# An encoder layer's bias-mask fill in four parts, and its output projection with operands two entries ahead, squares on ScalarE, sums by matmuls and other PSUM banks

## The chip, the cores and the metric

The kernel runs on one core of a Trainium2 chip. The metric is the device time of one execution in microseconds (us), as a median over several runs.

Engines are named as the profile names them: PE is TensorE (PEld its weight loads), DVE is VectorE, ACT is ScalarE, POOL is GpSimd, SP is SyncE, which issues the DMAs. PSUM, into which PE writes, has eight banks, numbered 0 to 7 here.

## The reference

One layer is computed for two batches that share the weights: 1024 tokens (`x_sample`) and 256 tokens (`x_prompt`), 1024 features, in float32.

```python
x = x + 0.5 * rmsnorm(swiglu(rmsnorm(x, ffn1_pre), ffn1_w_gu, ffn1_w_down), ffn1_post)
h = rmsnorm(x, mix_pre)
qa, ka, va, qb, kb, vb = jnp.split(h @ w_in, ...)
oa = window_gqa(rope(qa), rope(ka), va, sink_a)          # A: +-128 tokens, 8 heads on 2 kv heads
ob = neighbourhood_attn(qb, kb, vb, rpb_b)               # B: 8 x 16 window of a 64-wide grid, relative bias
mix = jnp.concatenate([rmsnorm(oa, out_norm_a), rmsnorm(ob, out_norm_b)], axis=-1) @ w_out
x = x + rmsnorm(mix, mix_post)
x = x + 0.5 * rmsnorm(swiglu(rmsnorm(x, ffn2_pre), ffn2_w_gu, ffn2_w_down), ffn2_post)
x = rmsnorm(x, final_norm)
```

`rmsnorm(x, g)` is `x * rsqrt(mean(x*x) + 1e-6) * g`. `swiglu(x)` is `(silu(x @ w_gate) * (x @ w_up)) @ w_down` with 2816 hidden features. Attention B adds a bias table where a key lies in the query's window and −1e30 elsewhere.

## The kernel before

**The numbers' form.** Each float32 operand of a product is split in two (`split`): a rounded part `h` and the rest `l`. A product is three matmuls, `h·h`, `h·l` and `l·h`, summed in PSUM. So each operand costs a copy on ACT and a subtraction on DVE ahead of PE.

**The order.** The program runs in stages: FFN1 (gate and up, then down), the mixer's projections and attentions A and B, the mixer output, FFN2 (gate and up, then down). Each engine has a queue of its own and works it off in order. The order on the queues is written by the code, by small planners (`pipe.start` gives a step's parts due times, `pipe.run` calls them between products) and by a tile scheduler that may move instructions within what the data allow. A tile's buffer is taken again only when its last reader is done, and a PSUM bank likewise.

**FFN gate and up** (`GateUp`). For each of 22 column blocks `f` and both row chunks, seven products (L324) go to four accumulators per chunk, with the tags `A0` to `A3` and `B0` to `B3` on banks 0 to 7. ACT and DVE turn them into hidden tiles `w` and `v` (two buffers each; L333 is the addition that starts `v`, L336 the copy that starts `u`). `store` writes them to DRAM as `hd` over SP (L357). While step `f` runs, `load` fetches the weights of a later one (L273), and `prep` splits them.

**The bias tables** (`bias_tables`). While FFN1 runs, each step `f` from 2 on calls one entry of a list, placed behind the last weight load of that step. Six `skew` steps write the tables `zd` and `zp` to DRAM. Then `fill_neg` writes the mask value −1e30 over all of `ttp` (2048 rows of 256 values, L500), and the steps after it copy table rows into `tt` (L488) and `ttp`.

**The down weights** (`wd_first`). Ahead of step 21 of either FFN the first weights of the down product are loaded (`rawd`) and split. The scheduler places these loads much earlier: beside step 8 in FFN1 and at the start of FFN2.

**Row factors.** `square` sums a row's squares on ACT (L194), `row_factor` makes `rsqrt(sum / 1024 + 1e-6)` of one or two such sums with small POOL instructions (L204 adds two sums, L206, L207). At the end of either FFN, two sums come together.

**The mixer output** (`MixOut`). Its work is ten entries, each two tiles of 128 rows for one attention: `(8,A), (0,A), (8,B), (2,A), (0,B), (4,A), (2,B), (6,A), (4,B), (6,B)`. `operands` loads the attention's output (tile `ml`, L984), makes `mh` by four ACT copies (L989), the squares by one DVE multiplication (L990) and two additions (L994, L995), and `ml` by four DVE instructions (L992). Two matmuls against a column of ones (L1000) give the rows' sums, and L1002 and L1003 make the row factor `ro` of them. `product` (L1015) makes a tile's half of 512 columns with twelve matmuls. `done` takes it from PSUM: for A an ACT copy into `y` (L1027), for B a DVE instruction that adds it to `y` (L1036). After B come the norms, the residual on POOL (L1042), the stores of `x2d` (L1044) and of the normalised tile `xnd` (L1048).

Entries 0 and 1 run inside the last attention head. `run` does entries 2 to 9, and starts the operands of entry n+1 with entry n. Beside entries 8 and 9 it calls steps of FFN2's preparation: `fetch2` loads tiles of `xnd` (L1316), `blocks` (L241 to L260) transposes and combines them, `gu.prep(0)` splits the first weights. The accumulators `y` have banks 0 to 4, the transposes and sums (tag `tr`) 6, 7 and 5.

Of the kernel before, what the change touches and what calls it, by code (L numbers as in the profile page):

```python
# [34 lines left out]
def third(t):  # L35
    return (t // 4, (t % 4) * 128) if t < 8 else (2, (t - 8) * 128)
# [31 lines left out]

def rstd(c, src_list, n):

    nc = c.nc
    ss = c.small.tile([128, 2], F32, name="ss")
    for i, s in enumerate(src_list):
        junk = c.junk.tile([128, s.shape[1]], BF16, name="junk", bufs=1)
        nc.scalar.activation(junk, s, AF.Square, accum_out=ss[:, i:i + 1])
    r = c.small.tile([128, 1], F32, name="rs")
    if len(src_list) == 2:
        s2 = c.small.tile([128, 1], F32, name="ss2")
        nc.gpsimd.tensor_tensor(s2, ss[:, 0:1], ss[:, 1:2], op=ALU.add)
    else:  # L80
        s2 = ss[:, 0:1]
    nc.gpsimd.tensor_scalar(r, s2, 1.0 / n, EPS, op0=ALU.mult, op1=ALU.add)
    nc.gpsimd.tensor_tensor(r, r, c.mhalf, op=ALU.pow)
    return r
# [17 lines left out]
def new_xt(c):  # L102
# [7 lines left out]
def norm_to_xt(c, x, gain, xt, t, xn=None):  # L110

    nc = c.nc
    r = rstd(c, [x], D)
    yield
    if xn is None:
        xn = c.work.tile([128, D], F32, name="xn")
    nc.vector.scalar_tensor_tensor(xn, x, r, gain, op0=ALU.mult, op1=ALU.mult)
    yield
    th, off = third(t)
    yield from transpose_split(c, xn, xt[0][th][:, :, off:off + 128], xt[1][th][:, :, off:off + 128])  # L120

# [69 lines left out]
def square(c, x, junk):  # L191

    ss = c.small.tile([128, 1], F32, name="ss")
    c.nc.scalar.activation(junk[:, :x.shape[1]], x, AF.Square, accum_out=ss)  # L194
    return ss


def row_factor(c, sums):

    nc = c.nc  # L200
    r = c.small.tile([128, 1], F32, name="rs")
    s = sums[0]
    if len(sums) == 2:
        nc.gpsimd.tensor_tensor(r, sums[0], sums[1], op=ALU.add)  # L204
        s = r
    nc.gpsimd.tensor_scalar(r, s, 1.0 / D, EPS, op0=ALU.mult, op1=ALU.add)  # L206
    nc.gpsimd.tensor_tensor(r, r, c.mhalf, op=ALU.pow)  # L207
    return r
# [168 lines left out]
class Down:  # L377
# [49 lines left out]
    def first_done(self, t, pool, junk):  # L427
        c, nc = self.c, self.c.nc
        ps = self.ps.pop(t)
        ss = self.ssq[:, t:t + 1]  # L430
        nc.scalar.activation(junk[:, :512], ps, AF.Square, accum_out=ss)
        y = pool.tile([128, 512], F32, name="y0")
        nc.vector.tensor_copy(y, ps)
        nc.sync.dma_start(self.y0d[t], y)
        self.ss[t] = ss
# [18 lines left out]
def bias_tables(c, G, rpb, cmask, neg, tt, ttp, zd, zp):  # L454
# [43 lines left out]

    def fill_neg():
        nc.sync.dma_start(ttp.rearrange("a n q h e k -> (a n q h) (e k)"), neg.to_broadcast([2048, 256]))  # L500

    steps = [lambda tau=tau, g=g: skew(g, tau) for g in range(2) for tau in range(3)]
    steps.append(lambda: (fill_neg(), fill(0, 0)))
    fills = [lambda a=a, rh=rh: fill(a, rh) for a in range(8) for rh in range(2)][1:]
# [411 lines left out]
class MixOut:  # L916
# [13 lines left out]
    def open(self):  # L930
# [7 lines left out]
        self.ones = wp.tile([128, 1], F32, name="ones")  # L938
        nc.gpsimd.memset(self.ones, 1.0)
        self.a = self.L.open("woa", 1)  # L940
# [32 lines left out]
    def prep(self, n):  # L973
        if n < len(self.seq):
            self.c.pipe.start(self.operands(*self.seq[n]), self.PREP)

    def operands(self, t, half):

        c, nc, a = self.c, self.c.nc, self.a
        lo = a.tile([128, 4, 256], F32R, name="ml", bufs=2)  # L980
        o = lo.bitcast(F32)
        src = self.oAd[:, :, t * 128:t * 128 + 256] if half == 0 else \
            (self.oBd[0][:, :, t * 128:t * 128 + 256] if t < 8 else self.oBd[1])
        nc.sync.dma_start(o, src.rearrange("j p t -> p j t"))  # L984
        yield
        hi = a.tile([128, 4, 256], F32R, name="mh", bufs=2)
        sq = a.tile([128, 4, 256], F32, name="sq")
        for j in range(4):
            nc.scalar.activation(hi[:, j], o[:, j], AF.Copy, scale=self.gon[:, 4 * half + j:4 * half + j + 1])  # L989
        nc.vector.tensor_tensor(sq, o, o, op=ALU.mult)  # L990
        for j in range(4):
            nc.vector.scalar_tensor_tensor(lo[:, j], o[:, j], self.gon[:, 4 * half + j:4 * half + j + 1], hi[:, j].bitcast(F32),  # L992
                                           op0=ALU.mult, op1=ALU.subtract)
        nc.vector.tensor_tensor(sq[:, 0:2], sq[:, 0:2], sq[:, 2:4], op=ALU.add)  # L994
        nc.vector.tensor_tensor(sq[:, 0], sq[:, 0], sq[:, 1], op=ALU.add)  # L995
        self.ops[t, half] = (hi, lo)
        yield
        ps = c.ps.tile([128, 2], F32, name="ssq", tag="tr")
        for i in range(2):
            nc.tensor.matmul(ps[:, i:i + 1], sq[:, 0, i * 128:i * 128 + 128], self.ones, start=True, stop=True)  # L1000
        r = c.small.tile([128, 2], F32, name="ro")
        nc.vector.tensor_scalar(r, ps, 1.0 / 512, EPS, op0=ALU.mult, op1=ALU.add)  # L1002
        nc.gpsimd.tensor_tensor(r, r, c.mhalf.to_broadcast([128, 2]), op=ALU.pow)  # L1003
        self.r[t, half] = r
# [45 lines left out]
    def run(self, G, beside):  # L1050

        c = self.c
        self.gmp = load_gain(c, G, self.g_mp, "ga")
        self.gf2 = load_gain(c, G, self.g_f2, "gb")
        for n in range(2, len(self.seq)):
            self.prep(n + 1)
            side = beside(n)
            for i in range(2):
                fill = []
                for s in range(2):  # L1060
                    fill.append((2.6, lambda s=s: self.product(n, i, s)))
                    fill += [(0.0, st) for st in side[2 * i + s::4]]
                c.pipe.run([[]], fill)
# [9 lines left out]
def encoder(tc, i, out_p, out_s):  # L1073
# [208 lines left out]
    def finish1(t, x, gain):  # L1282
# [7 lines left out]
        for _ in transpose_split(c, xn, state["xt"][0][th][:, :, off:off + 128], state["xt"][1][th][:, :, off:off + 128]):  # L1290
# [142 lines left out]
```

## Time and profile before

| | us |
|---|---|
| median of 3 runs | 2430.55 (2429.84 to 2431.99) |
| the profiled execution | 2433.46 |
| its span, from first to last instruction | 2431.4 |
| FFN1 gate and up, one step undisturbed | 24.63 |
| FFN1 gate and up, longest step | 42.66 |
| entries 2 to 9 of the mixer output (1419.0 to 1534.6 in the span) | 115.6 |
| from there to FFN2's second step (1534.6 to 1619.6) | 85.0 |

The profile's mean granted clock of PE was 0.983 of full speed. A line of the profile names engine, program line and operation with `output<-inputs`, counts (`x`), and times; in a timeline the first two numbers are the start in us from the span's start and the duration in us, and square brackets hold the idle time before the instruction and what ended it. In a row of windows each engine has its busy time and, in brackets, its instructions; the last three numbers are the granted clock, the DMA engines' busy share and GB/s.

### The profile page before, as it was taken

What the parts mean: (1) busy time and instruction counts of PE and PEld (TensorE: products, weight loads), DVE (VectorE), ACT (ScalarE), POOL (GpSimd) and SP (SyncE); (2) the same over time, 40 slices, a digit from 0 to 9 for tenths busy, and PEclk for the clock granted to TensorE, in tenths of its full rate; (3) what the DMA queues carried; (4) which work ended last, traced back from release to release, by engine and by line L of the source; (5) the groups of instructions that cost most, each with busy time, mean ns of one, the idle gap of its engine ahead of it and who ended that gap; (6) DMA issues with size and microseconds to landing.
All of it is one profiled execution on the core that took longest, in us unless ns stands there. A gap on an engine that the chain in (4) does not pass through costs nothing. (4 is left out here: it accounts for less than half of the span.)

```text
span 2431.4 us, 36273 instructions
## 1 busy us (share of the span) xinstructions
PE 2316.0 (95%) x13538; PEld 2111.2 (87%) x13538; DVE 1354.0 (56%) x2489; ACT 929.9 (38%) x1927; POOL 398.3 (16%) x568
## 2 busy tenths in 40 slices
PE   6999799999999998999999898799999999999997
PEld 5999799999778886888888777699999999978876
DVE  7565445464542552598655866665555555553344
ACT  5322222222442332587655744432222222342222
POOL 6000000000000111586433425600000000000011
PEclk9999899999999998999999999899999999999999
DMA  4244734631564443322432545332222222363544
GB/s 135 67 104 104 119 100 106 133 97 56 174 195 149 168 169 113 85 59 55 120 97 84 171 149 180 127 95 72 70 72 62 80 62 81 114 221 120 178 166 139
DMA packets 308463, 282.37 MB, mean 116 GB/s; under 512 B 64768, under 2 KB 248448, under 8 KB 308288
## 3 DMA queue, kind: packets, MB, share of 16 engines
q1 hardware_dynamic: 308288, 280.06, 40.1%
q8 instruction: 107, 1.75, 0.3%
q14 instruction: 68, 0.56, 0.1%
HBM read 207.51 MB, written 75.24 MB: 116 GB/s over the span
## 5 line engine op out<-in xcount | busy, mean ns | idle before, releaser
L324 PE MATMUL gups<-xh,ah 128*128 128x256 f32 (+1 forms) x2464 | 765.6, 311 | 31.8 <-DVE v L333 19.9
L324 PE MATMUL gups<-xh,al 128*128 128x256 f32 (+1 forms) x2464 | 763.3, 310 | 0.0
L324 PE MATMUL gups<-xl,ah 128*128 128x256 f32 (+1 forms) x2464 | 762.9, 310 | 0.0
L425 PE MATMUL dps<-wd,hh 128*128 128x512 f32 x1760 | 545.9, 391 | 4.7 <-ACT wd L63 2.6
L324 PEld LDWEIGHTS gups<-xh,ah 128*128 128x128 f32 x2464 | 470.1, 191 | 36.2 <-DVE v L333 21.6
L324 PEld LDWEIGHTS gups<-xh,al 128*128 128x128 f32 x2464 | 469.6, 191 | 0.6 <-DVE al L66 0.2
L324 PEld LDWEIGHTS gups<-xl,ah 128*128 128x128 f32 x2464 | 470.1, 191 | 0.0
L425 PEld LDWEIGHTS dps<-wd,hh 128*128 128x128 f32 x1760 | 328.7, 188 | 78.7 <-ACT wd L63 5.2
L425 PE MATMUL dps<-wd,hl 128*128 128x512 f32 x880 | 344.6, 392 | 2.2 <-DVE hl L66 2.0
L66 DVE TENSOR_TENSOR hl<-hl,hh 128x768 fp32r<-128x768 f32 (+1 forms) x160 | 142.3, 890 | 241.2 <-ACT hh L63 228.3
L204 POOL TENSOR_TENSOR rs<-ssq,ss 128x1 f32<-128x1 f32 x20 | 8.7, 434 | 1435.4 <-ACT junk L194 1435.4
L63 ACT ACTIVATE hh<-hl 128x768 fp32r<-128x768 f32 (+1 forms) x160 | 126.7, 793 | 269.1 <-DMA hl<-hd 240.5
L425 PEld LDWEIGHTS dps<-wd,hl 128*128 128x128 f32 x880 | 165.1, 188 | 43.3 <-DVE hl L66 9.7
L63 ACT ACTIVATE ah<-s 128x512 fp32r<-128x512 f32 x176 | 110.9, 630 | 230.6 <-PE gups L324 150.6
L66 DVE TENSOR_TENSOR al<-s,ah 128x512 fp32r<-128x512 f32 x176 | 121.5, 690 | 89.9 <-ACT ah L63 88.8
L554 PE MATMUL pj<-xh,mh 128*128 128x512 f32 (+1 forms) x432 | 162.2, 376 | 1.9 <-ACT mh L63 1.9
L554 PE MATMUL pj<-xh,ml 128*128 128x512 f32 (+1 forms) x432 | 155.9, 361 | 0.0
L554 PE MATMUL pj<-xl,mh 128*128 128x512 f32 (+1 forms) x432 | 155.5, 360 | 0.0
L577 POOL TENSOR_TENSOR sb<-sb,rc 128x384 f32<-128x384 f32 (+1 forms) x160 | 126.2, 809 | 154.8 <-DVE rc L575 138.7
L351 ACT ACTIVATE u<-u 128x256 f32<-128x256 f32 x88 | 41.4, 471 | 259.4 <-DVE u L333 255.5
L63 ACT ACTIVATE ah<-raw 128x512 fp32r<-128x512 f32 x132 | 83.1, 629 | 136.7 <-PE gups L324 125.3
L333 DVE TENSOR_TENSOR u<-u,gups 128x384 f32<-128x384 f32 (+1 forms) x176 | 85.5, 486 | 71.7 <-PE gups L324 70.1
(157 smaller groups left out, 3148.7 us busy)
## 6 DMA issues: line engine op xcount, KB each, us to landing
raw<-in_ffn_w_gu_dram SPq DMA_DIRECT2D x88, 512.0 KB, 3.9
hl<-hd SPq DMA_DIRECT2D x80, 384.0 KB, 3.6
hl<-hd SPq DMA_DIRECT2D x80, 320.0 KB, 3.4
rawd<-in_ffn_w_down_dram SPq DMA_DIRECT2D x88, 256.0 KB, 3.0
tab<-tt SPq DMA_DIRECT2D x24, 384.0 KB, 3.5
hd<-w SPq DMA_DIRECT2D x44, 192.0 KB, 2.1
hd<-v SPq DMA_DIRECT2D x44, 192.0 KB, 2.2
tt<-zd SPq DMA_DIRECT2D x16, 384.0 KB, 7.1
```

Source lines behind the costliest of these rows:

```text
L63: nc.scalar.activation(hi, src, AF.Copy)
L66: (lo_eng or nc.vector).tensor_tensor(lo, src, hi.bitcast(F32), op=ALU.subtract)
L204: nc.gpsimd.tensor_tensor(r, sums[0], sums[1], op=ALU.add)
L324: nc.tensor.matmul(ps, w[:, k, :], x[:, k, :], start=new and k == 0 and m == 0, stop=k == 3 and m == 2, skip_group_check=not new)
L333: nc.vector.tensor_tensor(out, x, ps, op=add)
L351: nc.scalar.activation(X["u"], X["u"], AF.Silu)
L425: nc.tensor.matmul(ps, a[:, i, :], b, start=f == 0 and m == 0, stop=f == NFF - 1 and m == 2)
L554: nc.tensor.matmul(ps[:, :n], w[:, kk, :], xs[th][:, kk, :], start=first, stop=last)
L577: nc.gpsimd.tensor_tensor(s, s, rc[:, i:i + 1].to_broadcast(list(s.shape)), op=ALU.mult)
```

## The change

**Row factors.** The 1/1024 goes into the squares (`scale=1/32` ahead of the square), so that one POOL instruction can add two sums and the constant. Two unused functions, `rstd` and `norm_to_xt`, are deleted.

**Bias mask fill.** It becomes four DMAs of 512 rows, called at the end of four of the six `skew` steps.

**Down weights.** `wd_first` is placed behind the last weight load, so that its loads, copies and subtractions stand beside steps 20 and 21.

**Mixer output.** Operands are prepared two entries ahead. The squares are one ACT instruction; eight matmuls against a column of 1/512 sum them, and the two DVE additions are gone. The operands of entries 3 and 6 take buffers of the tile `x` in another pool. `y` gets banks 2 to 5, `tr` 6, 7, 0 and 1.

**FFN2's preparation.** `gu.prep(0)` is called in steps beside entries 2 to 7, and eight instead of twelve steps of `blocks` beside each of entries 8 and 9.

```diff
@@ square, row_factor
-    c.nc.scalar.activation(junk[:, :x.shape[1]], x, AF.Square, accum_out=ss)
+    c.nc.scalar.activation(junk[:, :x.shape[1]], x, AF.Square, scale=1 / 32, accum_out=ss)
...
-    s = sums[0]
-    if len(sums) == 2:
-        nc.gpsimd.tensor_tensor(r, sums[0], sums[1], op=ALU.add)
-        s = r
-    nc.gpsimd.tensor_scalar(r, s, 1.0 / D, EPS, op0=ALU.mult, op1=ALU.add)
+    nc.gpsimd.tensor_scalar(r, sums[0], sums[1] if len(sums) == 2 else 0.0, EPS, op0=ALU.add, op1=ALU.add)
@@ bias_tables
-    def fill_neg():
-        nc.sync.dma_start(ttp.rearrange("a n q h e k -> (a n q h) (e k)"), neg.to_broadcast([2048, 256]))
-
-    steps = [lambda tau=tau, g=g: skew(g, tau) for g in range(2) for tau in range(3)]
-    steps.append(lambda: (fill_neg(), fill(0, 0)))
+    def fill_neg(a):
+        nc.sync.dma_start(ttp[a].rearrange("n q h e k -> (n q h) (e k)"), neg.to_broadcast([512, 256]))
+
+    steps = [lambda tau=tau, g=g: (skew(g, tau), fill_neg(2 * g + tau - 1) if tau else None) for g in range(2) for tau in range(3)]
+    steps.append(lambda: fill(0, 0))
@@ MixOut.open, prep, operands, run
-        nc.gpsimd.memset(self.ones, 1.0)
+        nc.gpsimd.memset(self.ones, 1.0 / 512)
...
-            self.c.pipe.start(self.operands(*self.seq[n]), self.PREP)
+            self.c.pipe.start(self.operands(*self.seq[n], n not in (3, 6)), self.PREP)
...
+        def tile(name):
+            if own:
+                return a.tile([128, 4, 256], F32R, name=name, bufs=2)
+            return c.G.tile([128, 4, 256], F32R, name=name, tag="x", bufs=3)
...
-        nc.vector.tensor_tensor(sq, o, o, op=ALU.mult)
+        nc.scalar.activation(sq, o, AF.Square)
...
-        nc.vector.tensor_tensor(sq[:, 0:2], sq[:, 0:2], sq[:, 2:4], op=ALU.add)
-        nc.vector.tensor_tensor(sq[:, 0], sq[:, 0], sq[:, 1], op=ALU.add)
...
-            nc.tensor.matmul(ps[:, i:i + 1], sq[:, 0, i * 128:i * 128 + 128], self.ones, start=True, stop=True)
+            for j in range(4):
+                nc.tensor.matmul(ps[:, i:i + 1], sq[:, j, i * 128:i * 128 + 128], self.ones, start=j == 0, stop=j == 3)
...
-        nc.vector.tensor_scalar(r, ps, 1.0 / 512, EPS, op0=ALU.mult, op1=ALU.add)
+        nc.vector.tensor_scalar(r, ps, EPS, None, op0=ALU.add)
...
+        self.prep(3)
         for n in range(2, len(self.seq)):
-            self.prep(n + 1)
+            self.prep(n + 2)
@@ encoder
-            wd_first(gu.down)
+            with tc.issue_after(gu.last_load.ins):
+                wd_first(gu.down)
...
-    c.ps.use(y=(0, 1, 2, 3, 4), tr=(6, 7, 5))
+    c.ps.use(y=(2, 3, 4, 5), tr=(6, 7, 0, 1))
...
-        return [lambda: next(side, None)] * 12 if n >= 8 else []
+        if n < 8:
+            return [lambda: next(first, None)]
+        return [lambda: next(side, None)] * 8
```

How this moves the rows shows at three places. The first is SP's queue in FFN1, where the mask fill (`ttp`) stood before; `hd` rows are the stores of `w` and `v`, `raw` and `rawd` weight loads, `tt<-zd` the first table fill.

```order
L386 DMA rawd<-in_ffn_w_down_dram 128x512
L273 DMA raw<-in_ffn_w_gu_dram 128x8x128
L500 DMA ttp<-in_neg_dram 2048x256
L488 DMA tt<-zd 16x24x256
L357 DMA hd_123<-w 128x3x128
L357 DMA hd_124<-v 128x3x128
```

Now a part stands in a `skew` step, between the load of its mask `cm` and the stores; no `rawd` row is near:

```order
L238 DMA raw<-in_ffn_w_gu_dram 128x8x128 x2
L439 DMA cm<-in_cmask_dram 96x512
L465 DMA ttp<-in_neg_dram 512x256
L322 DMA hd_123<-w 128x3x128
L445 DMA zd<-z 96x16x32
L322 DMA hd_124<-v 128x3x128
```

So each part of the fill stands ahead of two stores, as the whole fill did, in four steps instead of one. The second place is PE's queue in the mixer output, in the middle of entry 3. Before, the sums of squares of entry 3 stood there:

```order
L1000 MATMUL ssq<-ones,sq 128x1 x2
L1015 MATMUL yps<-woh_14129,mh 128x512
L1015 MATMUL yps<-wol_14130,mh 128x512
L1015 MATMUL yps<-woh_14129,ml 128x512
L1015 MATMUL yps<-woh_14133,mh 128x512
L1015 MATMUL yps<-wol_14134,mh 128x512
L1015 MATMUL yps<-woh_14133,ml 128x512
L1015 MATMUL yps<-woh_14147,mh 128x512
```

Now two groups of eight stand there, that of entry 3 and, after six products, that of entry 4:

```order
L969 MATMUL ssq<-ones,sq 128x1 x8
L984 MATMUL yps<-woh_14122,mh 128x512
L984 MATMUL yps<-wol_14123,mh 128x512
L984 MATMUL yps<-woh_14122,ml 128x512
L984 MATMUL yps<-woh_14126,mh 128x512
L984 MATMUL yps<-wol_14127,mh 128x512
L984 MATMUL yps<-woh_14126,ml 128x512
L969 MATMUL ssq<-ones,sq 128x1 x8
```

From entry 4 on, the sums of an entry stand in the middle of the entry ahead of it, half an entry before its first product. The third place is SP's queue where the operands of entry 9 are loaded (`ml` from `oBd`); `x2d` and `xnd` are the stores of tiles 2 and 3, `x1` the load of a residual.

```order
L1044 DMA x2d3_80<-x1_15090 128x1024
L1048 DMA xnd2_89<-x1_15024 128x1024
L984 DMA ml_15190<-oBd1024_150 128x4x256
L1048 DMA xnd3_90<-x1_15090 128x1024
L1033 DMA x1_15393<-x1d5_72 128x1024
```

And in the changed kernel:

```order
L1013 DMA x2d3_80<-x1_15165 128x1024
L1017 DMA xnd2_89<-x1_15101 128x1024
L1017 DMA xnd3_90<-x1_15165 128x1024
L1002 DMA x1_15436<-x1d5_72 128x1024
L954 DMA ml_15150<-oBd1024_150 128x4x256
```

The load now stands behind the last store of tile 3, which comes from entry 6, and behind a residual's load.

More of the change, by code (lines that the diff above doesn't have):

```diff
@@ L66, in split @@
     (lo_eng or nc.vector).tensor_tensor(lo, src, hi.bitcast(F32), op=ALU.subtract)
[L69 to L84, printed above, removed]
 def transpose_split(c, xn, hi, lo):
@@ L107, in new_xt @@
     return xh, xl
[L110 to L120, printed above, removed]
 def load_gain(c, pool, src, name, scale=None, n=D):
@@ L430, in first_done @@
         ss = self.ssq[:, t:t + 1]
-        nc.scalar.activation(junk[:, :512], ps, AF.Square, accum_out=ss)
+        nc.scalar.activation(junk[:, :512], ps, AF.Square, scale=1 / 32, accum_out=ss)
         y = pool.tile([128, 512], F32, name="y0")
@@ L974, in prep, with operands @@
         if n < len(self.seq):
-            self.c.pipe.start(self.operands(*self.seq[n]), self.PREP)
-    def operands(self, t, half):
+            self.c.pipe.start(self.operands(*self.seq[n], n not in (3, 6)), self.PREP)
+    def operands(self, t, half, own):
         c, nc, a = self.c, self.c.nc, self.a
-        lo = a.tile([128, 4, 256], F32R, name="ml", bufs=2)
+        def tile(name):
+            if own:
+                return a.tile([128, 4, 256], F32R, name=name, bufs=2)
+            return c.G.tile([128, 4, 256], F32R, name=name, tag="x", bufs=3)
+        lo = tile("ml")
         o = lo.bitcast(F32)
@@ L985, in operands @@
         yield
-        hi = a.tile([128, 4, 256], F32R, name="mh", bufs=2)
+        hi = tile("mh")
         sq = a.tile([128, 4, 256], F32, name="sq")
@@ L1322, in early @@
             yield from gu.blocks(p, *fetch2(p))
-        yield from gu.prep(0)
-        gu.load(1)
     side = early()
+    first = gu.prep(0)
     def beside(n):
@@ L1331, in beside @@
             gu.open_chunk(0, R.open("xbA", 1))
-        return [lambda: next(side, None)] * 12 if n >= 8 else []
+        if n < 8:
+            return [lambda: next(first, None)]
+        return [lambda: next(side, None)] * 8
     mo.run(G, beside)
+    for _ in first:
+        pass
+    gu.load(1)
     for _ in side:
@@ L1360, in encoder @@
         if f == NFF - 1:
-            wd_first(gu.down)
+            with tc.issue_after(gu.last_load.ins):
+                wd_first(gu.down)
         gu.run(f)
```

## The prediction

> **What bounds the kernel now.** I read the page first, then the waits of TensorE (PE), then the timeline of the first instruction of each FFN step, then windows by stage, and last the rows around each wait. The page's engine row:
>
> ```profile
> span 2431.4 us, 36273 instructions
> PE 2316.0 (95%) x13538; PEld 2111.2 (87%) x13538; DVE 1354.0 (56%) x2489; ACT 929.9 (38%) x1927; POOL 398.3 (16%) x568
> ```
>
> PE is busy 2316.0 of 2431.4 us, so 115.4 us are idle. The change takes no matmul away and adds some; it can only gain from idle time and from time at half clock. The waits of PE (sum, times, longest) that its edits touch:
>
> ```profile
> PE gups L324 <- DVE v L333: 19.9, 6, 15.0
> PE yps L1015 <- DVE ml L992: 13.3, 6, 6.3
> PE gups L324 <- DVE y L1036: 6.8, 1, 6.8
> ```
>
> The first lies in FFN1. The first `u` of each FFN step marks the step's period:
>
> ```profile
> 203.49 0.39 ACT L336 ACTIVATE u<-gups 128x256 f32<-128x256 f32 x1 [0.37 <-PE gups L324]
> 228.12 0.38 ACT L336 ACTIVATE u<-gups 128x256 f32<-128x256 f32 x1 [0.37 <-PE gups L324]
> 254.36 0.38 ACT L336 ACTIVATE u<-gups 128x256 f32<-128x256 f32 x1 [0.37 <-PE gups L324]
> 297.02 0.39 ACT L336 ACTIVATE u<-gups 128x256 f32<-128x256 f32 x1 [0.37 <-PE gups L324]
> 321.65 0.38 ACT L336 ACTIVATE u<-gups 128x256 f32<-128x256 f32 x1 [0.38 <-PE gups L324]
> ```
>
> The periods are 24.63, 26.24, 42.66 and 24.63 us. The step of 42.66 is 18.03 too long. What sits in it, from the timelines of SyncE (SP) and VectorE (DVE) and from the list of DMA issues (KB, us to landing):
>
> ```profile
> 250.45 0.64 SPq L500 DMA_DIRECT2D ttp<-in_neg_dram  x1
> 263.57 5.58 SPq L357 DMA_DIRECT2D hd<-v  x1
> 287.68 0.56 DVE L333 TENSOR_TENSOR v<-u,gups 128x384 f32<-128x384 f32 x1 [16.58 <-DMA hd<-v]
> ttp<-in_neg_dram SPq DMA_DIRECT2D x1, 2048.0 KB, 34.4
> hd<-v SPq DMA_DIRECT2D x44, 192.0 KB, 2.2
> ```
>
> The fill of 2 MB is issued at 250.45 and takes 34.4 us to land, until about 284.9. The store of `v`, whose median is 2.2 us, is issued at 263.57 behind it and lets DVE go on only at 287.68, 24 us later: it has waited out the fill in the DMA engines. DVE cannot overwrite `v`, the banks stay full, and PE stands.
>
> The other two waits lie in the mixer output. The windows cut it where entry 2 and where FFN2's first product begin:
>
> ```profile
> core 0: us, PE busy (x) PEld busy (x) DVE busy (x) ACT busy (x) POOL busy (x), PEclk, DMA share, GB/s
> 1350.00:1419.00 69.00, 59.37 (x339) 49.83 (x337) 52.70 (x115) 45.08 (x105) 27.68 (x25) 0.95 0.48 154
> 1419.00:1534.60 115.60, 103.20 (x473) 83.76 (x471) 79.81 (x115) 48.03 (x93) 57.73 (x54) 0.96 0.51 170
> 1534.60:1619.60 85.00, 68.33 (x435) 65.22 (x435) 57.37 (x84) 34.67 (x63) 27.79 (x24) 0.90 0.40 134
> ```
>
> PE is idle 9.6, 12.4 and 16.7 us there, 38.7 in all. Inside these, the stretches at a granted clock of 0.50:
>
> ```profile
> 1393.40:1400.20 6.80, 5.77 (x15) 4.61 (x16) 4.62 (x8) 4.98 (x13) 4.12 (x5) 0.50 0.06 19
> 1434.40:1437.80 3.40, 3.40 (x8) 2.75 (x9) 3.40 (x7) 0.37 (x1) 0.00 (x0) 0.50 0.83 279
> 1475.40:1482.20 6.80, 5.33 (x13) 4.17 (x14) 6.03 (x10) 3.09 (x7) 0.91 (x2) 0.50 0.75 248
> 1536.80:1547.00 10.20, 5.60 (x26) 5.63 (x27) 7.76 (x7) 3.83 (x7) 6.56 (x7) 0.50 0.41 155
> 1564.10:1570.90 6.80, 5.56 (x26) 5.16 (x26) 4.58 (x8) 4.04 (x8) 5.05 (x4) 0.50 0.38 115
> ```
>
> Work at 0.50 takes twice its time, so half of PE's busy time is lost: 2.9, 1.7, 2.7, 2.8 and 2.8 us, 12.9 in all. So 38.7 + 12.9 = 51.6 us are the most that these stages hold. The waits beside the slow stretches:
>
> ```profile
> 1394.43 0.79 PE L1015 MATMUL yps<-woh,mh 128*128 128x512 f32 x1 [2.23 <-ACT y L1027]
> 1434.34 0.77 PE L1015 MATMUL yps<-woh,ml 128*128 128x512 f32 x1 [1.54 <-DVE ml L992]
> 1476.87 0.80 PE L1015 MATMUL yps<-woh,ml 128*128 128x512 f32 x1 [6.30 <-DVE ml L992]
> 1541.40 0.55 PE L324 MATMUL gups<-xh,ah 128*128 128x256 f32 x1 [6.77 <-DVE y L1036]
> ```
>
> Waits of 2.23 and of 1.54 us already stand beside a half clock here. The Trainium skill, "TensorE: Matmul & The Clock Gate", section "Part 1: The HAM clock gate", gives the half clock only after an idle window of about 3.4 us, and by it alone my short new waits below would cost 3.4 us less (a sum of 2395.2). The trace speaks for charging them, and I do.
>
> **The change part by part.** The sum is made against the profiled execution, 2433.46 us (2.06 us lie around its span); the median of the runs shown is 2430.55, and the same differences go to that.
>
> *Bias mask fill.* Four parts of 512 KB go out in four steps, each behind one skew step's loads. A part lands, by its share of the 34.4 us, in about 8.6 us. It goes out where the fill did, 13.1 us ahead of the store of `v` (250.45 and 263.57), and so has landed before that store. If it came just ahead of a store instead, it would hold it up by 8.6; in the stalled step DVE came for `v` 24.1 − 16.6 = 7.5 us after the store's issue, which leaves 5.3 beyond the usual 2.2, so 3.3 would show, 13.2 for four parts. I take 0.15 a part, 0.6 (0 to 13.2): −18.0 + 0.6 = −17.4. The Trainium skill, "DMA: Bandwidth & Descriptors", section "Bandwidth", speaks against the split: it asks for 1 MB or more per DMA and measures 6.15 us for 1 MB, by which (my estimate) the whole fill would land in about 13 us and could not stall this step. The row has 34.4 us, so I follow the row; the rule is the ground of rival C.
>
> *Loads of the down weights.* They leave the step of 26.24 us, which is 1.61 too long, for the last two steps of either FFN, where the same five copies and five subtractions lie beside PE's products. Cover gone, the same 1.6 us is due at each end (0 to 3.2 in all); PE is the only engine near full there, so I take 0.5 each: −1.61 + 1.0 = −0.6.
>
> *Row factors.* One GpSimd (POOL) addition falls away. It lies on the path only at the two FFN ends:
>
> ```profile
> 2420.76 0.19 POOL L204 TENSOR_TENSOR rs<-ssq,ss 128x1 f32<-128x1 f32 x1 [4.94 <-ACT junk L194]
> 2421.04 0.19 POOL L206 TENSOR_SCALAR rs<-rs 128x1 f32<-128x1 f32 x1
> ```
>
> Start to start that is 0.28 us: −0.6 for two (0 to −0.6). Elsewhere the work on other tiles hides it.
>
> *Sums of squares.* Eight matmuls instead of two:
>
> ```profile
> 1484.46 0.50 PE L1000 MATMUL ssq<-ones,sq 128*128 128x1 f32 x4
> 1484.82 0.49 PE L1015 MATMUL yps<-woh,mh 128*128 128x512 f32 x1
> 1495.85 0.50 PE L1000 MATMUL ssq<-ones,sq 128*128 128x1 f32 x4
> ```
>
> Two matmuls leave four records and hold PE for 0.36 us, so six more cost 1.1 us an entry, always on PE: 2.2 for entries 0 and 1, 8.8 for entries 2 to 9. The second and third row also give an undisturbed entry's length, 11.0 us. DVE loses a multiplication and two additions an entry, ACT gains a square:
>
> ```profile
> L989 ACT ACTIVATE mh<-ml,gon x40: 491/495/520, 1374.3 to 1510.1; 128x256 fp32r<-128x256 f32 x40
> L194 ACT ACTIVATE junk<-y x10: 1049/1058/1059, 1427.7 to 1545.1; 128x1024 bf16<-128x1024 f32 x10
> L990 DVE TENSOR_TENSOR sq<-ml x10: 1209/1218/2519, 1374.0 to 1511.5; 128x1024 f32<-128x1024 f32 x10
> L1042 POOL TENSOR_TENSOR x<-x,y x10: 2337/2517/3370, 1431.5 to 1552.3; 128x1024 f32<-128x1024 f32 x10
> ```
>
> By the rows L194 and L990 the square moves 1.06 us to ACT, of whose 115.6 us only 48.03 are busy, and takes 1.22 from DVE; both lie beside PE.
>
> *Entries 0 and 1* (1350 to 1419). Attention's own waits stay. The wait of 2.23 with its half clock of 2.9, and 1.9 of the `ml` waits (13.3 in the whole run, 11.3 of them after 1419), make 7.1. The operands' earlier start doesn't reach entry 0, so I take half: −3.5 + 2.2 = −1.3 (−4.9 to +2.2).
>
> *Entries 2 to 9* (1419 to 1534.6). Operands start two entries ahead, and the idle 12.4 with half clocks of 1.7 and 2.7 goes: −16.8. The matmuls add 8.8. Left over I put 1.0. Two new waits come. `ssq(n)` now stands in the middle of entry n−1, so PE can wait there for ACT's square with all later products queued behind it. For entry 4, the square stands on ACT behind three copies of entry 5's operand, 3 × 0.495 = 1.5 us. For entry 9, the load now stands on SP behind entry 7's x2 and normalised stores. Its price:
>
> ```profile
> 1507.33 0.32 SPq L1048 DMA_DIRECT2D xnd<-x  x1
> ml<-oBd SPq DMA_DIRECT2D x5, 512.0 KB, 4.4
> ```
>
> That store is the second tile of entry 6, whose middle is the row at 1484.46: 22.9 us later. Load 4.4, four copies 2.0 and the square 1.06 end 30.3 us after that middle. PE comes to `ssq(9)` after two entries and one group of squares, 22.0 + 1.5 = 23.5. That is 6.8 late at worst, none at best if the chain behind the store (its additions of 2.34 to 3.37 us on POOL) shortens with its waits; I take 3.0. Each wait with 1.7 of half clock beside it (the 1434.40 stretch): 1.5 + 3.0 + 3.4 = +7.9. Sum: −16.8 + 8.8 + 1.0 + 7.9 = +0.9 (−8 to +6).
>
> *Into FFN2* (1534.6 to 1619.6). FFN2's first products take banks 0 and 1. Before, `y` used them, and the wait of 6.77 was for entry 9's evacuation; now `y` has 2 to 5, and 6.8 + 2.8 of half clock = −9.6. Of the other 12.7 (16.7 + 5.6 − 9.6) the wider spread of FFN2's preparation takes about a quarter, −3.4; the last tiles' chain through POOL keeps the rest: −13.0 (−22.3 to 0).
>
> Sum: −17.4 − 0.6 − 0.6 − 1.3 + 0.9 − 13.0 = −32.0. The profiled execution would be 2401.5 us, the median 2398.6.
>
> **The rivals.**
> A, the mixer output yields nothing net. The path there is the chain through DVE, POOL and the x stores, which the change leaves as it is, and the `ssq` waits eat the bank's 9.6. For it: the 6.30 wait at 1476.87 ends on DVE, where the operands of the next entry stand behind a chain that waits on POOL. Against: the bank wait goes whatever happens there. Only fill, loads and row factors count, −18.6: 2412.0.
> B, all idle and half-clock time of the three stages goes: −18.6 − (51.6 − 11.0) = −59.2: 2371.4. Against: part of it is attention's, which is not touched.
> C, the split doesn't end FFN1's stall, because the table fills or the stores behind it are what is slow and not the 2 MB: 2398.6 + 18.0 = 2416.6. Against: the store waits until 2.8 us after the fill's landing.
> D, slower. Every one of the eight `ssq` groups makes PE wait for ACT's square as long as the longest `ml` wait, 6.3 + 2.7 of half clock = 9.0, together 72; without my two waits the sum is −32.0 − 7.9 = −39.9, so +32: about 2463. It decides from 39.9 / 8 = 5.0 us an entry. Against: ACT is busy 48.03 of 115.6 us, and a copy queue of 2.0 is all that stands ahead of most squares.
>
> **How the numbers follow.** Forecast 0.60 (its own range 2389 to 2407), A 0.19, B 0.10, C 0.05, D 0.04, none of these 0.02. A measurement of this kernel tells about 0.2%, 4.9 us, from no change. The range 2380 to 2418 holds the forecast with the bounds of its stages (the bank wait kept raises it by 9.6, fill parts that show by 12.6), A and C, and the part of B that stops short; the rest of B, and D, are out. All but D are faster by over 0.2%: faster 0.94, same 0.02, slower 0.04.
>
> **What would show it.** Right: no step of FFN1 over 27 us; the `gups` wait on `y` gone; the `ml` waits in the mixer output down to about a microsecond, with waits of `ssq` on the squares at entries 4 and 9. Wrong: a `v` step that still lasts over 35 us; a wait of `ssq` of 5 us or more at most entries; the stretch from entry 2 to FFN2's second step as long as before or 40 us shorter.

## The result

| | before | changed |
|---|---|---|
| median, us | 2430.54 (2429.84 to 2431.99) | 2410.38 (2407.82 to 2410.93) |
| profiled execution, us | 2433.46 | 2410.93 |
| its span, us | 2431.4 | 2409.2 |

The ratio is 0.9914, with a 95% interval of 0.9897 to 0.9931. The change gains 20 us; 32 were forecast, and 18.6 in rival A. So the sign and the wide range of 2380 to 2418 held, and the time lies beside A's 2412.0, above the forecast's own range of 2389 to 2407.

**FFN1.** The first `u` of each step in the changed kernel, in the same stretch as before (L301 is the old L336):

```profile
226.73 0.38 ACT L301 ACTIVATE u<-gups 128x256 f32<-128x256 f32 x1 [0.37 <-PE gups L289]
251.37 0.38 ACT L301 ACTIVATE u<-gups 128x256 f32<-128x256 f32 x1 [0.38 <-PE gups L289]
276.00 0.38 ACT L301 ACTIVATE u<-gups 128x256 f32<-128x256 f32 x1 [0.38 <-PE gups L289]
300.63 0.38 ACT L301 ACTIVATE u<-gups 128x256 f32<-128x256 f32 x1 [0.37 <-PE gups L289]
```

Every period is 24.63 or 24.64 us: the two long steps (26.24 and 42.66) are gone, 19.6 us together. The list of DMA issues has the four parts:

```profile
ttp<-in_neg_dram SPq DMA_DIRECT2D x4, 512.0 KB, 10.2
```

They land in 10.2 us at the median, a little slower for their size than the whole (2048 KB in 34.4). The stores behind a part do show it. The first part, the stores of `w` and `v` behind it, and the times to landing of these two stores (shortest, median, longest):

```profile
124.81 0.64 SPq L465 DMA_DIRECT2D ttp<-in_neg_dram  x1
126.31 0.39 SPq L322 DMA_DIRECT2D hd<-w  x1
130.91 3.92 SPq L322 DMA_DIRECT2D hd<-v  x1
DMA to landing us min/median/max: 7.8/8.5/9.3
```

Behind the other three parts they take 7.1 to 9.4 us, against a median of 2.1 and 2.2 over all such stores. No step gets longer by it: DVE next writes that `v` at 145.11, 14 us after the store's issue, and PE has no wait from 120 to 250.

**The mixer output.** I measure this stage from the start of the last projection matmul (`pj`, inside the last head) to the start of FFN2's product number 300, counted from 0; both are found in every kernel. Windows of before, cut at entry 2's sums and at the end of entry 9:

```profile
1363.18:1418.89 55.71, 46.08 (x243) 37.48 (x242) 42.29 (x87) 35.95 (x80) 24.02 (x21) 0.94 0.47 159
1418.89:1534.60 115.71, 103.31 (x473) 83.86 (x471) 79.81 (x115) 48.03 (x93) 57.73 (x54) 0.96 0.51 170
1534.60:1611.70 77.10, 60.42 (x385) 57.32 (x385) 51.80 (x74) 31.62 (x58) 27.79 (x24) 0.89 0.39 132
```

And of the changed kernel at the same places:

```profile
1344.67:1400.58 55.91, 48.57 (x267) 40.79 (x266) 34.07 (x78) 38.63 (x83) 23.48 (x21) 0.94 0.49 163
1400.58:1520.85 120.27, 112.62 (x571) 95.48 (x570) 74.38 (x97) 56.89 (x104) 55.94 (x57) 0.96 0.52 173
1520.85:1588.80 67.95, 59.03 (x385) 55.83 (x383) 44.91 (x67) 26.91 (x49) 25.84 (x21) 0.92 0.30 103
```

The first column behind the bounds is the length, the second PE's busy time, the third number from the end its granted clock. The stage went from 248.5 to 244.1 us: +0.2, +4.6 and −9.2. PE's idle time, length less busy time, fell from 38.7 to 23.9, and its busy time rose by 10.4: the sums of squares add some 13.4 (worked out below), and the time at half clock shrank only from 34.1 to 27.3 us, which gives back about 3.4. FFN1's gate and up took 19.9 us less, from first to last product, and the span 22.2 less; so the rest of the program took 2.1 longer, which is within its scatter. The waits of PE in this stage:

```profile
PE ssq L969 <- ACT sq L960: 6.5, 1, 6.5
PE tr L206 <- DVE y L1005: 4.1, 1, 4.1
PE tr L206 <- POOL t L213: 2.7, 1, 2.7
PE yps L984 <- DVE ml L962: 2.4, 2, 1.3
```

The wait of `gups` on `y` is gone, and the waits for `ml` fell from 13.3 to 2.4. Two waits are new: one for the squares of entry 9, and one of FFN2's transposes for `y`.

### The profile page after: what moved, and what is told of

It reads as the page before. It is cut to its first block, busy times and chain, and to the rows that moved or that the text cites. A ratio compares the mean times of both kernels' runs of the same rounds, so it can differ in the third digit from the quotient of the medians.

```text
span 2409.2 us, 36473 instructions
## 1 busy us (share of the span) xinstructions
PE 2321.3 (96%) x13658; PEld 2119.2 (88%) x13658; DVE 1336.0 (55%) x2459; ACT 940.9 (39%) x1937; POOL 393.0 (16%) x548
## 4 chain that ended last, share of the span: by engine, by line
PE 46%; DMA 5%; DVE 4%; POOL 2%; ACT 2%; issue 2%; SPq 0%; DVEq 0%; POOLq 0%; ACTq 0%
PE gups L289 21%; PE pj L519 9%; PE dps L390 6%; PE yps L984 3%; DMA hl<-hd 2%; PE s_ps L548 2%; PE pt L558 2%; DMA rawd<-in_ffn_w_down_dram 1%; ACT junk L163 1%; PE ssq L969 1%; PE o_ps L675 1%; DMA out_dram<-xr 1%; DVE stk L66 1%; POOL rs L172 1%; DVE sb L531 0%
## 5 line engine op out<-in xcount | busy, mean ns | idle before, releaser
L171 POOL TENSOR_SCALAR rs<-ssq,ss 128x1 f32<-128x1 f32 x20 | 9.5, 475 | 1422.7 <-ACT junk L163 1422.7
```

## The experiments

Times are medians with the ratio to the kernel before on the same chip. "The stage" is the one above, from one profiled execution each. Its scatter shows where its code is the same: 248.5, 247.4 and 252.1 with the mixer output of before (before, b_fill4, b_fill4_one); 244.1, 244.5 and 243.3 with that of the changed kernel (changed, a_again, a_wd_old).

| kernel | ratio (95% interval) | stage, us | PE busy | PE idle |
|---|---|---|---|---|
| before | 1 | 248.5 | 209.8 | 38.7 |
| changed | 0.9914 (0.9897 to 0.9931) | 244.1 | 220.2 | 23.9 |
| a_again, the same | 0.9900 (0.9886 to 0.9915) | 244.5 | 219.8 | 24.8 |
| a_ssq9 | 0.9896 (0.9881 to 0.9911) | 242.8 | 219.2 | 23.6 |
| a_banks_old | 0.9902 (0.9888 to 0.9916) | 251.7 | 225.9 | 25.8 |
| a_y45 | 0.9904 (0.9890 to 0.9917) | 245.4 | 221.2 | 24.2 |
| a_prep1 | 0.9905 (0.9891 to 0.9918) | 241.7 | 218.2 | 23.5 |
| a_ssq2 | 0.9866 (0.9853 to 0.9880) | 237.4 | 205.7 | 31.8 |
| a_dve_sums | 0.9909 (0.9894 to 0.9923) | 245.8 | 210.6 | 35.1 |
| a_add_dve | 0.9882 (0.9865 to 0.9899) | 241.8 | 219.6 | 22.2 |
| a_best | 0.9849 (0.9835 to 0.9862) | 228.2 | 206.6 | 21.6 |

Only a_ssq2 and a_best are clear of the changed kernel's interval; for the others the stage and its waits have to speak, within their scatter.

### b_fill4: the fill's four parts alone

```diff
@@ before, bias_tables (fill_neg as in the change)
...
-    steps = [lambda tau=tau, g=g: skew(g, tau) for g in range(2) for tau in range(3)]
-    steps.append(lambda: (fill_neg(), fill(0, 0)))
+    steps = [lambda tau=tau, g=g: (skew(g, tau), fill_neg(2 * g + tau - 1) if tau else None) for g in range(2) for tau in range(3)]
+    steps.append(lambda: fill(0, 0))
```

> The kernel before with the four-part mask fill alone. Theory: the fill's DMA in one piece is FFN1's stall, and four pieces in four steps end it at no cost: 2430.5 - 18.0 = 2412.5 us, the longest FFN1 step 26 us (the down weights' step). Rival C: the table fills behind it are what is slow: no change, 2430 us, and a step of over 40 us stays.

2416.33 us, ratio 0.9942 (0.9930 to 0.9954). Rival C falls: the stall goes with the split. But the step before it is longer:

```profile
226.93 0.38 ACT L336 ACTIVATE u<-gups 128x256 f32<-128x256 f32 x1 [0.38 <-PE gups L324]
257.66 0.39 ACT L336 ACTIVATE u<-gups 128x256 f32<-128x256 f32 x1 [0.38 <-PE gups L324]
282.29 0.38 ACT L336 ACTIVATE u<-gups 128x256 f32<-128x256 f32 x1 [0.38 <-PE gups L324]
```

The down weights' step takes 30.73 us, 4.5 more than before, and the next one 24.63. PE's wait in that step:

```profile
PE gups L324 <- ACT u L336: 3.0, 1, 3.0
```

The down weights' copies stand in ACT's queue ahead of `u`, in the step that a part of the fill shares, and wait there for their loads:

```profile
238.36 0.63 ACT L63 ACTIVATE wd<-rawd 128x512 fp32r<-128x512 f32 x1 [8.17 <-DMA rawd<-in_ffn_w_down_dram]
240.71 0.63 ACT L63 ACTIVATE wd<-rawd 128x512 fp32r<-128x512 f32 x1 [1.72 <-DMA rawd<-in_ffn_w_down_dram]
```

The first of these loads goes out at 234.71, 7.8 us after the step's first `u`; in the kernel before it goes out at 232.68, 4.6 us after.

### b_fill4_one: four parts at the old place

```diff
@@ before, bias_tables (fill_neg as in the change)
...
-    steps.append(lambda: (fill_neg(), fill(0, 0)))
+    steps.append(lambda: ([fill_neg(a) for a in range(4)], fill(0, 0)))
```

> The kernel before with the mask fill in four parts that are all issued at the old place, one behind the other. If it matters how much is in flight ahead of the store, this stalls as before: 2430 us, a step of 42 to 43 us. If the size of one DMA matters, the stall goes as with the parts spread: 2412 us.

2433.36 us, ratio 1.0011 (1.0002 to 1.0020).

```profile
252.36 0.38 ACT L336 ACTIVATE u<-gups 128x256 f32<-128x256 f32 x1 [0.37 <-PE gups L324]
295.73 0.38 ACT L336 ACTIVATE u<-gups 128x256 f32<-128x256 f32 x1 [0.38 <-PE gups L324]
```

Its four parts in the list of DMA issues:

```profile
ttp<-in_neg_dram SPq DMA_DIRECT2D x4, 512.0 KB, 20.7
```

The step of 43.37 us is there again. Between these two kernels the size of one DMA decides nothing; what is in flight ahead of the stores does.

### a_wd_old: the down weights' loads where they were

```diff
@@ changed, encoder, both FFNs
-            with tc.issue_after(gu.last_load.ins):
-                wd_first(gu.down)
+            wd_first(gu.down)
```

> The changed kernel with the down weights' first loads where they were before. By the prediction it is 0.6 us slower than the changed kernel (a step of 26.2 us returns, 1.6, and 0.5 at each FFN's end goes): 2411.0. By the two traces the moved loads cost more than they gave (first down products of FFN1 2.2 us and of FFN2 1.3 us later, the last gate and up steps 1.1): 3 us faster, 2407.4.

2414.31 us, ratio 0.9931 (0.9916 to 0.9946). The sum of FFN1's gate and up, from first to last product, is 580.2 us, against 576.8 and 576.4 in two executions of the changed kernel and 596.7 before:

```profile
226.73 0.38 ACT L301 ACTIVATE u<-gups 128x256 f32<-128x256 f32 x1 [0.38 <-PE gups L289]
255.25 0.38 ACT L301 ACTIVATE u<-gups 128x256 f32<-128x256 f32 x1 [0.37 <-PE gups L289]
```

The long step is back with 28.52 us, 3.9 too long. So moved loads and split fill belong together: beside the split, the move is worth some 3.5 us in FFN1. The later down products, on which I had built the expectation that the move costs more than it gives, are within the scatter: from the last FFN1 gate and up product to the last `pj` matmul it took 740.4 us here, 745.8 and 743.2 in two executions of the changed kernel, and 740.7 and 741.1 in a_add_dve and a_ssq9, whose code is that of the changed kernel up to there. The whole time of this kernel doesn't settle it: its interval overlaps that of the changed kernel.

### a_ssq9: entry 9's sums half an entry later

```diff
@@ changed, prep
-            self.c.pipe.start(self.operands(*self.seq[n], n not in (3, 6)), self.PREP)
+            self.c.pipe.start(self.operands(*self.seq[n], n not in (3, 6)), self.PREP if n < 9 else self.PREP[:2] + [(4, 8, 0.0)])
```

> The changed kernel with the sums of squares of entry 9 in the middle of entry 9, as before the change, instead of in the middle of entry 8; all others stay. Theory: the wait of 6.5 us and the half clock behind it (about 2.8) are a loss of their own: 9 us faster, 2401 us. Rival: the last tiles' chain through DVE, POOL and the stores sets FFN2's start, and the wait moves to a transpose or to a bank: 2408 to 2410 us.

2405.00 us, ratio 0.9896 (0.9881 to 0.9911). PE's waits in the stage:

```profile
PE tr L206 <- DVE xl L209: 4.9, 1, 4.9
PE tr L206 <- POOL rs L171: 2.7, 1, 2.7
PE tr L206 <- DVE y L1005: 2.6, 1, 2.6
```

The wait of 6.5 is gone and the stage is only 1.4 to 1.8 us shorter: transposes between the products wait instead, for DVE (4.9) and POOL (2.7). The rival holds for the stage. The median is 5 us lower. The profiled executions lie 7.2 us apart, but 4.7 of these lie ahead of the stage, which begins at 1340.0 instead of 1344.7, and there the code is the same.

### a_banks_old and a_y45: the banks

```diff
@@ changed, encoder: a_banks_old
-    c.ps.use(y=(2, 3, 4, 5), tr=(6, 7, 0, 1))
+    c.ps.use(y=(0, 1, 2, 3, 4), tr=(6, 7, 5))
@@ changed, encoder: a_y45
-    c.ps.use(y=(2, 3, 4, 5), tr=(6, 7, 0, 1))
+    c.ps.use(y=(4, 5, 2, 3), tr=(6, 7, 0, 1))
```

> The changed kernel with the banks of before for the mixer output (y on 0 to 4, tr on 6, 7, 5). By the prediction's term the wait of FFN2's first products returns with its half clock, 9.6 us: 2420. By the trace of the changed kernel, where a transpose waits 4.1 us for y's banks 4 and 5 instead, the banks gave only the difference: 6.8 - 4.1 = 2.7 us, 2413.

> The changed kernel with the same four banks for y in another order (4, 5, 2, 3), so that the last tile of entry 9 leaves 2 and 3, and FFN2's first transposes (banks 4 and 5) wait only for the tile before it. If the bank is what the transposes wait for: 4.1 us faster, 2406. Rival: the last tiles' chain through DVE and POOL sets when FFN2's step 0 can go on, and the wait only gets another name: 2409 to 2410.

a_banks_old: 2407.48 us, ratio 0.9902 (0.9888 to 0.9916), not slower. Its profiled execution has a stage of 251.7 with 25.8 us idle and 225.9 busy at a mean clock of 0.92, with 41.0 us at half clock against 27.3 in the changed kernel; it was the slowest of its four (2411.58). The old banks cost 1.9 us of idle time there, and the half clock differs between executions. No wait of `gups` on `y` came back, so the new banks are not needed to end it. What the banks are worth stays open; the 9.6 us of the prediction are excluded by the median.

a_y45: 2408.36 us, ratio 0.9904 (0.9890 to 0.9917), stage 245.4. The wait for `y` is gone, and others stand in its place:

```profile
PE gups L289 <- DVE xl L209: 2.4, 1, 2.4
PE gups L289 <- DVE v L298: 2.1, 2, 2.0
```

### a_prep1: operands one entry ahead

```diff
@@ changed, run
-        self.prep(3)
...
-            self.prep(n + 2)
+            self.prep(n + 1)
```

> The changed kernel with the operands prepared one entry ahead, as before the change; squares, matmuls and banks stay. If the two entries' lead is what ended the waits for ml (11.3 us and 4.4 of half clock in before), they return, and the wait of entry 9's sums (6.5 and 2.8) goes: +15.7 - 9.3, 2417 us. Rival: the last tiles' chain sets the end of the mixer output either way: 2409 to 2411, with the waits at other places.

2408.35 us, ratio 0.9905 (0.9891 to 0.9918); stage 241.7. PE's waits there:

```profile
PE yps L984 <- ACT y L996: 4.5, 2, 2.9
PE tr L206 <- DVE xl L209: 2.8, 1, 2.8
PE yps L984 <- DVE ml L962: 2.4, 2, 1.3
```

With one entry's lead the waits for `ml` stay at 2.4. So the lead isn't needed to end them; it gave no time that shows. By the stages of these executions it cost 2 to 3 us, but stages of the same code lie up to 4.7 apart. PE now waits for ACT's copies of `y` instead (4.5) and for DVE.

### a_ssq2: two matmuls for the sums

```diff
@@ changed, operands
-            for j in range(4):
-                nc.tensor.matmul(ps[:, i:i + 1], sq[:, j, i * 128:i * 128 + 128], self.ones, start=j == 0, stop=j == 3)
+            nc.tensor.matmul(ps[:, i:i + 1], sq[:, 0, i * 128:i * 128 + 128], self.ones, start=True, stop=True)
```

> The changed kernel with two matmuls an entry for the sums of squares instead of eight; the sums then cover only the first quarter of the squares, three quarters are left out. Eight matmuls hold PE for 1.7 us in the changed kernel's trace, two held it for 0.36: 13.4 us less in ten entries. If PE's own time sets the end of the mixer output: 2397 us. If the last tiles' chain does, the sums cost only where nothing waits: 2405 to 2409.

2399.41 us, ratio 0.9866 (0.9853 to 0.9880); the stage in one window:

```profile
1342.83:1580.24 237.41, 205.66 (x1099) 176.38 (x1098) 153.71 (x241) 121.90 (x236) 105.09 (x99) 0.94 0.46 155
```

PE's busy time fell by 14.6 us and its idle time rose by 7.8, to 31.8. By the stage, both theories hold in part: some 7 of the sums' 14 us are on the path, and the other half fills time in which PE would wait for other engines. The medians say more, 11 us less than the changed kernel and 10 less than a_again, near the theory that PE's own time counts. Part of that lies outside the stage, where the code is the same. So the share on the path lies between half and four fifths.

### a_dve_sums: squares and sums on DVE

```diff
@@ changed, operands
-        nc.scalar.activation(sq, o, AF.Square)
+        nc.vector.tensor_tensor(sq, o, o, op=ALU.mult)
...
+        nc.vector.tensor_tensor(sq[:, 0:2], sq[:, 0:2], sq[:, 2:4], op=ALU.add)
+        nc.vector.tensor_tensor(sq[:, 0], sq[:, 0], sq[:, 1], op=ALU.add)
```

The two matmuls are those of a_ssq2, now over complete sums.

> The changed kernel with squares and their sums on DVE as before (one multiplication and two additions an entry, two matmuls), while operands stay two entries ahead and the banks as changed. If DVE's relief ended the waits for ml (with one entry's lead they had not come back), they return here, some 11 us, less 13.4 us of matmuls: 2405 to 2410 us. If the lead ended them, they stay away: 2397 to 2401 us.

2411.08 us, ratio 0.9909 (0.9894 to 0.9923); PE's waits in the stage:

```profile
PE tr L206 <- DVE y L1006: 7.4, 2, 4.4
PE yps L985 <- ACT y L997: 5.1, 2, 2.9
PE ssq L970 <- DVE sq L965: 5.1, 2, 4.9
PE yps L985 <- DVE ml L962: 4.9, 3, 1.9
```

Without DVE's relief the waits for `ml` are 4.9 us, where the kernel before has 13.3; without the lead (a_prep1) they are 2.4, as in the changed kernel, and with the old banks 5.1. Taking one edit away brings little of them back, so which one ended them isn't shown; the lead is the least needed. Waits for `y` stand here in their place. The 5.1 for the squares is not new: 4.9 of it is entry 9's wait, 6.5 in the changed kernel. PE does 9.6 us less and idles 35.1 us, 11.2 more: the exchange of DVE's squares for ACT's and PE's is worth 1 or 2 us at most.

### a_add_dve: the last residual additions on DVE

```diff
@@ changed, done
-        nc.gpsimd.tensor_tensor(x1, x1, y, op=ALU.add)
+        (nc.vector if half and 2 <= t < 8 else nc.gpsimd).tensor_tensor(x1, x1, y, op=ALU.add)
```

> The changed kernel with the residual additions of the B tiles 2 to 7 on DVE instead of POOL (2.4 us each there, DVE's norm instruction beside it 3.4 us instead of 1.28). If the last tiles' chain through DVE and POOL sets FFN2's start, it gets 1.2 us shorter a tile on the addition and up to 2.1 on the norm: 3 to 8 us faster, 2402 to 2407. If PE's sums and waits on the squares set it: 2409 to 2411.

2405.74 us, ratio 0.9882 (0.9865 to 0.9899); stage 241.8. The wait for entry 9's squares fell to 4.6, since its load stands behind a store that now comes earlier (the load goes out 23.7 us after the middle of entry 6, in the changed kernel 25.6). That is the low end of what was expected from the last tiles' chain, and the interval overlaps the changed kernel's.

### a_again and a_best

a_again is the changed kernel once more, on the chip of a_dve_sums and a_add_dve. a_best joins what had looked useful.

```diff
@@ changed, with the edits of a_prep1 and a_add_dve: open, operands (the sums' tile has four columns; the row factor reads every second)
-        self.ones = wp.tile([128, 1], F32, name="ones")
-        nc.gpsimd.memset(self.ones, 1.0 / 512)
+        one = wp.tile([128, 2], F32, name="one")
+        nc.gpsimd.memset(one, 1.0 / 512)
+        self.ones = wp.tile([128, 2], F32R, name="ones")
+        nc.vector.tensor_copy(self.ones, one)
...
-        sq = a.tile([128, 4, 256], F32, name="sq")
+        sq = a.tile([128, 4, 256], F32R, name="sq")
...
-                nc.tensor.matmul(ps[:, i:i + 1], sq[:, j, i * 128:i * 128 + 128], self.ones, start=j == 0, stop=j == 3)
+                nc.tensor.matmul(ps[:, 2 * i:2 * i + 2], sq[:, j, i * 128:i * 128 + 128], self.ones, start=j == 0, stop=j == 3)
...
```

> The changed kernel unaltered, once more, to see how far its executions scatter beside its variants on one chip: 2408 to 2411 us, and in the trace 244 us from the last projection matmul (pj) to FFN2's 300th product, give or take 3.

> The changed kernel with operands one entry ahead, the residual additions of the B tiles 2 to 7 on DVE, and the squares and the column of 1/512 in the rounded format fp32r (two equal columns), so that a sum's matmul leaves one record instead of two. By the stage from the last projection matmul to FFN2's 300th product (244.3 us in the changed kernel): one entry's lead 241.7, additions on DVE 241.8, and half of the 6.7 us that six matmuls an entry cost. If the gains add up: 244.3 - 2.6 - 2.5 - 3.4 = 235.8 us, 2401 in all. If they are one gain, found three times: 241, 2406.

a_again: 2409.17 us, ratio 0.9900 (0.9886 to 0.9915), stage 244.5. a_best: 2395.53 us (2391.58 to 2396.79), ratio 0.9849 (0.9835 to 0.9862), clear of the changed kernel's interval, stage 228.2. The gains add up, and there are 7.6 us more than that. The stage in one window, and PE's longest wait in it:

```profile
1342.10:1570.27 228.17, 206.60 (x1139) 176.84 (x1138) 153.34 (x248) 122.96 (x236) 93.28 (x93) 0.98 0.49 162
```

```profile
PE yps L986 <- ACT y L998: 5.5, 3, 2.8
```

PE's busy time is about that of a_ssq2, its idle time is the lowest of all, and the granted clock is 0.98 instead of 0.94: 10.2 us of the stage run at half clock instead of 27.3. No wait in it is over 2.8 us; that the shorter waits are the cause was not tested by itself. A group of eight sums, in the changed kernel and in a_best, with the product behind it:

```profile
1447.51 1.84 PE L969 MATMUL ssq<-ones,sq 128*128 128x1 f32 x16
1449.21 0.49 PE L984 MATMUL yps<-woh,mh 128*128 128x512 f32 x1
```

```profile
1439.60 0.95 PE L971 MATMUL ssq<-ones,sq 128*128 128x2 f32 x8
1440.41 0.49 PE L986 MATMUL yps<-woh,mh 128*128 128x512 f32 x1
```

1.70 us against 0.81: the rounded format leaves one record a matmul instead of two. Which of the three edits brings the 7.6 us was not taken apart; the sums' 0.89 us for ten entries are 8.9 instead of the 3.4 that I had counted, and 17.1 us less at half clock are worth up to 8.5.

## Why the prediction was right, and where not

**Fill: right in what it ends, lucky in what the parts cost.** The term was −17.4, the step lost 18.0. That the 2 MB hold the store was shown by b_fill4 and b_fill4_one. But the 0.6 for the parts rested on a wrong path. "It goes out where the fill did, 13.1 us ahead of the store of `v`": 12.3 of these 13.1 us SP spent behind the fill, on issuing `tt` and `hd<-w` (6.26 and 6.03 us; in b_fill4 0.58 and 0.38), so they were part of the stall. A part goes out 1.5 us ahead of the store of `w` and 5.6 to 6.1 ahead of that of `v`, which then takes 7 or 8 us. The price put on this case, 3.3 us a part, did not come either, because DVE needs that `v` only 14 us after the store's issue and not 7.5 us after it, as in the stalled step. In b_fill4 a part does cost 4.5 us, through the down weights' loads, a way that the prediction doesn't have. The rule of the Trainium skill, "DMA: Bandwidth & Descriptors", section "Bandwidth", to batch to 1 MB or more would have kept one DMA. This transfer does move somewhat faster whole, 60 KB a microsecond against 50 for a part, but the stores behind it cost the 18 us.

**Down weights: right alone, but not independent.** The step's 1.6 us went. Its price at the ends came too: in FFN1 the step that now has the loads and the one behind it last 25.84 and 23.96 us, 0.5 more than two of 24.63, in FFN2 26.09 and 23.97, 0.8 more (0.5 each were forecast). The prediction priced the two edits apart; with the fill split and the loads left in place the step is 3.9 to 4.5 us too long, so their terms don't add as written.

**Row factors** were too small to be seen in a run; no experiment isolates them.

**The mixer output: the failing part.** Forecast −13.4 (−1.3, +0.9 and −13.0), measured −4.4 (+0.2, +4.6 and −9.2). Step by step:

- *Sums of squares.* 1.1 us more an entry was forecast, 1.70 − 0.36 = 1.34 measured, 13.4 instead of 11.0 in ten entries. That the sum counted all of them beside the waits is a second fault, of the other sign: by the stage of a_ssq2, about half stands in waiting time.
- *"Operands start two entries ahead, and the idle 12.4 with half clocks of 1.7 and 2.7 goes."* The size was right: in entries 2 to 9 PE idles 7.7 us, and 1.2 without the wait of `ssq(9)`; 1.0 was forecast. The cause named was not: the waits for `ml` stay away without the lead (a_prep1), and some of them return without DVE's relief (a_dve_sums), which the prediction booked under "both lie beside PE".
- *`ssq(9)`.* Forecast 3.0 with 1.7 of half clock, "6.8 late at worst". It was 6.5. The rows of SP, ACT and PE in the changed kernel:

```profile
1484.94 0.32 SPq L1017 DMA_DIRECT2D xnd<-x  x1
1485.84 0.73 SPq L954 DMA_DIRECT2D ml<-oBd  x1
1491.49 1.70 ACT L959 ACTIVATE mh<-ml,gon 128x256 fp32r<-128x256 f32 x4 [6.70 <-DMA ml<-oBd]
1493.10 1.04 ACT L960 ACTIVATE sq<-ml 128x1024 f32<-128x1024 f32 x1
1494.19 3.58 PE L969 MATMUL ssq<-ones,sq 128*128 128x1 f32 x16 [6.47 <-ACT sq L960]
```

  The mechanism is the one forecast: store, load, copies, square, sums. Its steps were longer: the square ends 33.9 us after the middle of entry 6 (1460.29), forecast 30.3; PE was there after 27.4, forecast 23.5. With the half clock beside it (7.91 us of work in 10.2) the wait is worth 10.4 where 4.7 were forecast; this is what made entries 2 to 9 longer than forecast, more than the sums did. The wait of entry 4 (1.5 and 1.7) didn't show. But a_ssq9 also shows that the wait's price is not its length: without it, the transposes wait for DVE and POOL, and the stage gains 1.4 to 1.8 us.
- *"Into FFN2", −13.0.* It was −9.2 here. The wait for the bank moved, from FFN2's products to its transposes, which use banks 4 to 7 from then on, and so stand behind `y` on 4 and 5 for 4.13 us:

```profile
1526.81 1.11 PE L206 MATMUL tr<-ident,x 128*128 128x128 f32 x4 [4.13 <-DVE y L1005]
```

  So of the bank's 9.6 about 2.5 came, 6.8 − 4.1 with nearly the same half clock, and with the old banks (a_banks_old) the wait of `gups` on `y` stays away as well. The rest of the stretch gave 6.7 instead of 3.4, and no run says by which edit. The stretch behind this wait runs at a granted clock of 0.50:

```profile
1527.00:1530.40 3.40, 3.40 (x17) 3.40 (x17) 0.80 (x1) 2.30 (x5) 3.15 (x5) 0.50 0.07 27
```

**The rivals.** A gave the nearest time. Its mechanism is half shown: four edits (a_ssq9, a_y45, a_prep1, a_banks_old) change the waits' names and, within the scatter, hardly the time, and in the stage of a_ssq2 half of what PE saves turns into waiting; but a_best shows that the chain is no fixed bound. B, C and D fell: 23.9 us of idle are left, the split ended the stall, and no `ssq` but entry 9's waits over 1.1 us. The waits of 6.47 and 4.13 us brought half clock, as I charged. That fits the idle window of about 3.4 us of the Trainium skill, "TensorE: Matmul & The Clock Gate", section "Part 1: The HAM clock gate", too; the waits of 1.54 and 2.23 us before, with half clock beside them, are shorter than that. A charge for every short wait is not borne out: in a_best two waits for ACT's `y`, of 2.48 us at 1448.63 and 2.82 at 1475.68, lie in stretches at a granted clock of 1.00.

**What stays open.** What the banks and the two entries' lead are worth within some 3 us; how much of the sums lies on the path; which edit ended the waits for `ml`; and which edit of a_best brings what: the cheaper sums, one entry's lead, or DVE's freedom beside POOL.

## What to carry to other kernels

Price a removed wait by what is late next on the same engines: where several engines hand tiles to each other in one chain, four waits could be removed here one at a time for little that is clear of the scatter. Look at a small operation's cost on the fullest engine first, and count its records: the sums of squares, a minor line of the change, were worth more than its waits. And a large transfer that delays others is split in time, not in size.

## What the runs showed of the hardware

DVE's norm instruction (two operands in SBUF) takes 1.28 us alone and 3.4 us when POOL's addition starts just before it:

```profile
1474.79 3.41 DVE L157 SCALAR_TENSOR_TENSOR x<-x,rs,gb 128x1024 f32<-128x1024 f32 x1 [0.76 <-POOL rs L172]
1483.62 1.29 DVE L157 SCALAR_TENSOR_TENSOR x<-x,rs,gb 128x1024 f32<-128x1024 f32 x1 [5.35 <-POOL rs L172]
```

```profile
1474.71 2.41 POOL L1011 TENSOR_TENSOR x<-x,y 128x1024 f32<-128x1024 f32 x1
```

POOL ends at 1477.12 and DVE 1.08 us later: it did most of its work after POOL, not beside it. All six such pairs from 1400 to 1560 take DVE 3.37 to 3.42 us, each ending 1.08 us after POOL; the four without POOL's addition take 1.28 or 1.29. The Trainium skill, "SBUF — State Buffer", section "Summary: rules for kernel authors", says that the second of two such instructions blocks fully until the first is done; this trace agrees, with 3.41 against 1.29 us.

Between executions of the same code, FFN1's down phase, the projections and the attention took 740.7 to 745.8 us (a_add_dve and the changed kernel). In the table the intervals of the ratios are 0.0027 to 0.0034 wide, 7 to 8 us, so a difference of 2 us can't be told from none.
